# Chunked SSD scan: two products moved from GpSimd to VectorE, and the decode steps' order constraint dropped

## The chip, the cores and the metric

One core of one Trainium2 chip. The metric is the device time of one execution of the whole program in microseconds; a kernel's time is the median of several runs. Everything is f32 in memory; the large products run on TensorE as three f32r products each (high by high, high by low, low by high part).

## The reference

One inference step of a hybrid decoder layer, for a prompt of 1024 positions and for 8 decode sequences of one position each. The part around the change is the SSD scan (24 heads of 64, 4 groups of B and C, state 64, chunks of 128 positions):

```python
    acum = jnp.cumsum(dtc * a.reshape(G, R), axis=2)
    ...
    y_diag = jnp.einsum('bclsgr,bcsgrp->bclgrp', mix, xc)
    chunk_states = jnp.einsum('bclgn,bclgr,bclgrp->bcgrpn', bc, decay_to_end * dtc, xc)
    chunk_decay = jnp.exp(acum[:, :, -1])
    def step(h, inp):
        cs, cd = inp
        return cd[..., None, None] * h + cs, h
    ...
    y_off = jnp.einsum('bclgn,bcgrpn,bclgr->bclgrp', cc, h_in, jnp.exp(acum))
    y = y_diag + y_off
```

The decode sequences do one step of the same recurrence on a state that is read from memory and written back. Before the scan stand a projection and a causal convolution of x, B and C; behind it the gate SiLU(z), a grouped norm, the pooling groups, the output projection and the feed-forward part.

## The kernel before, in words

The program has a startup, the scans of the prompt beside the input projection (`ssd_phase`, line 754), a stage with the rest of the gates and the pooling groups, the output projection, and the feed-forward part with its up and down projection. The scans lie between about 137 and 396 us of the profiled execution.

`ssd_phase` makes a queue of small tasks and lets the projection's tiles (`conv_tile`, `gate_tile`, products L159 to L161) call `between` ahead of each of their three column blocks; `between` takes tasks from the queue by a credit. So the scan's steps lie between the projection's products. There are two scans, `ssd_tasks(0)` and `ssd_tasks(1)`, with 12 heads and two groups of B and C each. A scan has eight chunks. `step(c)` applies chunk c (`apply`), prepares the products of chunk c + 1 (`turn`) and the exponentials of chunk c + 2 (`decay`).

- `decay` (line 529) loads the cumulated logarithms of the decay in a broadcast form, clamps them on VectorE (L538), and takes 12 exponentials on ScalarE (called through L188) for `mix`. For c > 0 it takes the exponentials `ce` too and multiplies them with C (L553, GpSimd). `mix` and `ce` have two buffers.
- `turn` (line 556) transposes B and x on TensorE (L565, L574), makes the product of C and B (L571), copies and scales them on VectorE (L575, L576, L578) and multiplies `mix` with the product of C and B on VectorE (L583, two per chunk).
- `apply` (line 588) makes the chunk's state on TensorE (L597, in the single bank pM), multiplies the old state with its decay (L606, GpSimd), adds the two (L610, VectorE), and makes the output in the banks pY from `mix` and x (L620) and from `ce` and the old state (L630). VectorE adds the skip term (L638).

`sample_tile` (line 653) is one decode step for two heads of all 8 sequences: it loads B and C (L662, when they change) and a state (L666), and does 13 or so small operations on GpSimd alone (L670 to L682, with the write of the state at L674). The tiles of a step have one buffer each, so the steps follow one another. Seven steps belong to `ssd_phase`: 0 to 2 are queued behind the first scan, 3 to 6 after chunks 0, 2, 4 and 6 of the second. The helper `sample` (line 796) puts all GpSimd instructions of a step behind `self.pl`, the last L606 traced so far. Five further steps lie in the next stage, without this. Other work of GpSimd in the scans: the low parts of the weights during the first scan (L141; VectorE does them in the second), small copies for the convolution (L494, L495, L511) and sums of the grouped norm (L714).

The order of the instructions on each engine is not written out by hand. A scheduler orders them when the program is built (`TileContext(nc, schedule_with_timeline_sim=True)`, line 1589), by an expected time at which each is ready; on the chip each engine then runs its list in that order. `behind(ins)` (line 175) adds an order to it: what is traced in its block and runs on the engine of `ins` is put behind `ins` in that engine's list. It is no wait for a result.

Of the kernel before, what the change touches and what calls it, by code (L numbers as in the profile page):

```python
# [13 lines left out]
ALU = mybir.AluOpType  # L14
# [4 lines left out]
P = 128  # L19
# [56 lines left out]
class Kernel:  # L76
    def __init__(self, ctx, tc, d):
        self.ctx, self.tc, self.nc, self.d = ctx, tc, tc.nc, d
        nc = self.nc
        pool = lambda name, bufs=1, **kw: ctx.enter_context(tc.tile_pool(name=name, bufs=bufs, **kw))  # L80
        self.const = pool("const")
        self.wpool = pool("weights")
        self.big = pool("big", 30)
        self.dram = pool("scratch", 1, space=DRAM)

        self.cst = self.const.tile([P, NCONST], F32, name="cst")
        self.mat = self.const.tile([P, NMAT], F32, name="mat")
        self.conv_st = self.const.tile([P, 16, 35], F32, name="conv_st")
        self.ones = self.const.tile([P, P], F32, name="ones")
        nc.vector.memset(self.ones, 1.0)  # L90
        self.zero = self.const.tile([P, P], mybir.dt.bfloat16, name="zero")
        nc.vector.memset(self.zero, 0.0)
        self.eps = self.const.tile([P, 1], F32, name="eps")
        nc.gpsimd.memset(self.eps, EPS)
        self.ident = self.mat[:, M_ID : M_ID + P]
        self.uid = 0
        self.lo_eng = nc.vector
        self.hooks = []
        self.pl = None
        self.tab = self.set = None  # L100
        self.table_set(EXPLN)

# [426 lines left out]
    def decay(self, q, c):  # L529

        nc = self.nc
        h0 = 12 * q
        mix = self.ph.tile([P, 12, P], F32, tag="mix", name=self.nm("mix"), bufs=2)
        src = lambda h, n, p: self.acd[c : c + 1, h * P : (h + n) * P].partition_broadcast(p)
        nc.sync.dma_start(mix.rearrange("p r l -> p (r l)"), src(h0, 12, P))
        hs = c * NH + h0

        nc.vector.scalar_tensor_tensor(  # L538
            out=mix, in0=self.acl[:, hs : hs + 12].unsqueeze(2).broadcast_to([P, 12, P]), scalar=80.0, in1=mix,
            op0=ALU.subtract, op1=ALU.max,  # L540
        )
        ce = None
        if c > 0:
            ce = self.ph.tile([P, 6, P], F32, tag="ce", name=self.nm("ce"), bufs=2)
            for g in range(2):
                rows = slice(64 * g, 64 * g + 64)
                nc.sync.dma_start(ce[rows].rearrange("p r l -> p (r l)"), src(h0 + 6 * g, 6, 64))
        for r in range(12):
            self.tables(mix[:, r], mix[:, r], AF.Exp, bias=self.acl[:, hs + r : hs + r + 1], scale=-1.0)
        if c > 0:  # L550
            self.tables(ce, ce, AF.Exp, scale=-1.0)
            cc = self.ctl[q][:, c * P : (c + 1) * P]
            nc.gpsimd.tensor_tensor(out=ce, in0=ce, in1=cc.unsqueeze(1).broadcast_to([P, 6, P]), op=ALU.mult)  # L553
        return mix, ce

    def turn(self, q, c, mix):
# [31 lines left out]
    def apply(self, q, c, mix, ce, xd, bT):  # L588

        nc = self.nc  # L590
        cols = slice(c * P, (c + 1) * P)
        h = self.hst.get(q)
        halves = [slice(0, 64), slice(64, 128)]
        pys = [self.bank("pY") for _ in range(2)]
        pst = self.bank("pM")
        for g, rows in enumerate(halves):
            nc.tensor.matmul(  # L597
                pst[rows, :384], bT[:, rows], xd[:, 1, 6 * g : 6 * g + 6].rearrange("p r x -> p (r x)"),
                start=True, stop=True,
            )  # L600
        h1 = self.ph.tile([P, 384], F32, tag="h", name=self.nm("h"), bufs=2)
        if c == 0:
            nc.scalar.activation(h1, pst[:, :384], AF.Copy)
        else:
            by_head = lambda t: t.rearrange("p (r x) -> p r x", x=64)
            self.pl = nc.gpsimd.tensor_tensor(  # L606
                out=by_head(h1), in0=by_head(h),
                in1=self.cd[:, c, q].unsqueeze(2).broadcast_to([P, 6, 64]), op=ALU.mult,
            ).ins
            nc.vector.tensor_tensor(out=h1, in0=h1, in1=pst[:, :384], op=ALU.add)  # L610
        self.hst[q] = h1
        if c == NCH - 1:
            nc.sync.dma_start(self.d["ssm_p"][q], h1)

        for g in range(2):
            for i in range(3):
                o = slice(i * P, (i + 1) * P)
                for j, out in enumerate(halves):
                    r = 6 * g + 2 * i + j
                    nc.tensor.matmul(  # L620
                        pys[g][out, o], xd[:, 0, r, :], mix[:, r, :], start=(i == 0), stop=(c == 0 and i == 2),
                        skip_group_check=True,
                    )

        for i in range(3 if c > 0 else 0):
            o = slice(i * P, (i + 1) * P)
            for j, out in enumerate(halves):
                r = 2 * i + j
                for g, rows in enumerate(halves):
                    nc.tensor.matmul(  # L630
                        pys[g][out, o], h[rows, r * 64 : (r + 1) * 64], ce[rows, r, :], start=False, stop=(i == 2),
                        skip_group_check=True,
                    )
        for g in range(2):
            for i in range(3):
                k = 6 * q + 3 * g + i
                t = self.xs[k][:, cols]
                nc.vector.scalar_tensor_tensor(  # L638
                    out=t, in0=t, scalar=self.c("dsk", k), in1=pys[g][:, i * P : (i + 1) * P],
                    op0=ALU.mult, op1=ALU.add,  # L640
                )
# [112 lines left out]
    def ssd_phase(self):  # L754
        nc, d = self.nc, self.d
        self.hst = {}
        self.tags = {"bc": ("bc", 1), "st": ("st", 1), "stt": ("stt", 1), "dx": ("dx", 2)}
        queue = []

        credit = [0.0, 0.0]  # L760

        def between():
            credit[0] += credit[1]
            while credit[0] >= 1.0 and queue:
                credit[0] -= 1.0
                queue.pop(0)()
            if not queue:
                credit[0] = 0.0

        def flush():  # L770
            while queue:
                queue.pop(0)()

        def ssd_tasks(q):
            dec, trn = {}, {}

            def start():
                dec[0] = self.decay(q, 0)

            def step(c):  # L780
                if c >= 0:
                    self.apply(q, c, *dec.pop(c), *trn.pop(c))
                if c + 1 < NCH:
                    trn[c + 1] = self.turn(q, c + 1, dec[c + 1][0])
                if c + 2 < NCH:
                    dec[c + 2] = self.decay(q, c + 2)
                if c == -1 and q == 0:
                    self.sample_bc(q)
                if q == 1 and c in (0, 2, 4, 6):
                    sample(3 + c // 2)  # L790

            queue.append(start)
            for c in range(-1, NCH):
                queue.append(lambda c=c: step(c))

        def sample(i):
            with self.behind(self.pl):
                self.sample_tile(i // 6, i)

        self.lo_eng = nc.gpsimd  # L800
        for n in range(1, 6):
            self.keep(n, self.conv_tile(n, n, None))
        ssd_tasks(0)
        credit[:] = 0.35, 0.6
        for n in (13, 15, 6, 7, 8, 9):
            self.keep(n, self.conv_tile(n, n, between))
        flush()
        self.lo_eng = nc.vector
        self.sample_bc(1)
        for i in range(3):  # L810
            queue.append(lambda i=i: sample(i))
        credit[1] = 0.7
        for n in (10, 11):
            self.keep(n, self.conv_tile(n, n, between))
        nc.sync.dma_start(d["conv_o"], self.conv_st)

        ssd_tasks(1)
        self.gate_tile(16, 0, between)
        credit[:] = 0.35, 0.6
        for i in range(1, 7):  # L820
            self.gate_tile(16 + i, i, between)
        flush()
        self.run_due()
# [789 lines left out]
```

## Time and profile before

| | |
|---|---|
| median of 3 runs | 1409.85 us (1405.99 to 1411.67) |
| profiled execution, its own time | 1407.76 us |
| its span, first to last instruction | 1406.0 us |
| mean granted clock of TensorE, share of full | 0.984 |
| VectorE busy | 991.2 us (70%) |
| ScalarE busy | 700.6 us (50%) |
| GpSimd busy | 561.5 us (40%) |

In the rows below PE is TensorE, PEld its weight load, DVE VectorE, ACT ScalarE, POOL GpSimd. L553 is line 553 of the kernel. A busy time is from an instruction's start to its end and includes what it lost to others while it ran. The names are the program's tiles, without buffer numbers: `ce` and `mix` are the exponentials, `h` the state, `wop` the parts of the weights, `pT`, `pM`, `pY` and `g` banks that TensorE writes.

### The profile page before, as it was taken

To read this page: it belongs to the slowest core of one execution; us is meant where nothing else is said; L and a number is where in the kernel's file an instruction comes from. 1 tells how busy PE (TensorE), PEld (TensorE's weight loads), DVE (VectorE), ACT (ScalarE), POOL (GpSimd) and SP (SyncE) were. 2 spreads that over 40 slices of the span, in tenths; PEclk is the share of its full clock that TensorE was granted. 3 is DMA by queue.
4 is the path that set the end of the run, shared out by engine and by line. 5 is a ranking of instruction groups with operands and counts; after the bars stand their busy time and mean duration, and the time that the engine had idled before them with its cause. 6 is when DMAs were issued, how large, how long until landed. Compare 5 with 4: busy or idle time off the path is not lost. (4 is left out here: it accounts for less than half of the span.)

```text
span 1406.0 us, 26779 instructions
## 1 busy us (share of the span) xinstructions
PE 1360.4 (97%) x10360; PEld 1312.9 (93%) x10360; DVE 991.2 (70%) x1453; ACT 700.6 (50%) x1408; POOL 561.5 (40%) x704
## 2 busy tenths in 40 slices
PE   8999999979999999999979999999999999999997
PEld 7799879968799999899979999999999999999997
DVE  6575898669865684844689877777776787567743
ACT  6346774546644451311456545554554465444452
POOL 4233465888668305774222212212222224214122
PEclk9999999989999999999999999999999999999999
DMA  6031235243331256675477877777777769657513
GB/s 248 1 108 38 93 118 168 81 142 116 94 104 62 74 192 209 214 253 178 152 204 148 210 205 193 187 207 183 185 187 201 196 207 328 225 185 235 180 55 121
DMA packets 117820, 228.09 MB, mean 162 GB/s; under 512 B 19884, under 2 KB 37116, under 8 KB 117692
## 3 DMA queue, kind: packets, MB, share of 16 engines
q1 hardware_dynamic: 73772, 130.21, 29.3%
q0 software_dynamic: 27056, 70.22, 19.8%
q10 hardware_dynamic: 16864, 25.95, 5.6%
q8 instruction: 81, 1.33, 0.4%
q14 instruction: 47, 0.39, 0.1%
HBM read 169.64 MB, written 45.15 MB: 153 GB/s over the span
## 5 line engine op out<-in xcount | busy, mean ns | idle before, releaser
L1118 PE MATMUL g<-op,wop 128*128 128x258 f32 x3696 | 446.9, 283 | 4.3 <-DVE op L1048 1.6
L1118 PEld LDWEIGHTS g<-op,wop 128*128 128x128 f32 x3696 | 445.3, 189 | 5.6 <-DVE op L1048 2.0
L140 ACT ACTIVATE wop<-raw 128x512 fp32r<-128x512 f32 (+1 forms) x208 | 125.9, 608 | 231.2 <-PE g L161 139.7
L1300 PE MATMUL g<-op,wop 128*128 128x258 f32 x1848 | 224.9, 283 | 1.6 <-ACT op L210 0.9
L159 PE MATMUL g<-hh,wop 128*128 128x344 f32 x696 | 226.1, 325 | 0.0
L160 PE MATMUL g<-hl,wop 128*128 128x344 f32 x696 | 225.3, 324 | 0.0
L1300 PEld LDWEIGHTS g<-op,wop 128*128 128x128 f32 x1848 | 222.5, 189 | 2.7 <-ACT op L210 1.1
L161 PE MATMUL g<-hh,wop 128*128 128x344 f32 x696 | 224.8, 323 | 0.0
L141 DVE TENSOR_TENSOR wop<-raw,wop 128x512 fp32r<-128x512 f32 (+1 forms) x186 | 159.7, 862 | 83.3 <-ACT wop L140 81.5
L140 ACT ACTIVATE wop<-s 128x512 fp32r<-128x512 f32 (+1 forms) x136 | 83.6, 620 | 137.6 <-PE g L1300 51.9
L1098 POOL DMA_DIRECT2D s<-s x44 | 37.7, 857 | 249.8 <-DVE wop L141 89.2
L159 PEld LDWEIGHTS g<-hh,wop 128*128 128x128 f32 x696 | 132.2, 190 | 1.2 <-issue 1.1
L161 PEld LDWEIGHTS g<-hh,wop 128*128 128x128 f32 x696 | 132.1, 190 | 1.2 <-issue 1.2
L160 PEld LDWEIGHTS g<-hl,wop 128*128 128x128 f32 x696 | 132.1, 190 | 0.5 <-issue 0.4
L1200 DVE SCALAR_TENSOR_TENSOR acc<-u,cst,acc 128x1048 f32<-128x1048 f32 x88 | 115.2, 1309 | 12.2 <-ACT acc L1198 10.6
L141 DVE TENSOR_TENSOR wop<-s,wop 128x512 fp32r<-128x512 f32 (+1 forms) x136 | 92.1, 682 | 36.5 <-ACT wop L140 34.1
L1178 DVE TENSOR_TENSOR u<-u,g 128x258 f32<-128x258 f32 (+2 forms) x176 | 58.0, 354 | 72.2 <-PE g L1118 67.6
L1175 ACT ACTIVATE u<-g 128x258 f32<-128x258 f32 (+2 forms) x220 | 69.6, 340 | 71.2 <-PE g L1118 71.2
L160 PE MATMUL g<-yl,wop 128*128 128x344 f32 x288 | 93.4, 325 | 3.2 <-DVE yl L211 3.2
L161 PE MATMUL g<-yh,wop 128*128 128x344 f32 x288 | 93.0, 323 | 0.0
L159 PE MATMUL g<-yh,wop 128*128 128x344 f32 x288 | 92.9, 323 | 0.0
L1270 POOL DMA_DIRECT2D g<-td x77 | 41.2, 539 | 123.1 <-DVE op L211 70.2
(276 smaller groups left out, 2333.9 us busy)
## 6 DMA issues: line engine op xcount, KB each, us to landing
s<-wup SPq DMA_DIRECT2D x88, 256.0 KB, 3.2
g<-td POOLq DMA_DIRECT2D x77, 258.0 KB, 4.5
raw<-wup SPq DMA_DIRECT2D x66, 256.0 KB, 4.1
raw<-win SPq DMA_DIRECT2D x58, 256.0 KB, 2.7
mix<-acd SPq DMA_DIRECT2D x16, 768.0 KB, 4.5
td<-acc ACTq DMA_DIRECT2D x22, 516.0 KB, 6.1
s<-wup POOLq DMA_DIRECT2D x44, 256.0 KB, 5.3
s<-s POOLq DMA_DIRECT2D x44, 256.0 KB, 3.9
```

The lines of the kernel that those rows point to most:

```text
L140: self.nc.scalar.activation(hi, raw[:, :w], AF.Copy)
L141: lo_eng.tensor_tensor(out=lo, in0=raw[:, :w], in1=hi.bitcast(F32), op=ALU.subtract)
L159: nc.tensor.matmul(ps[:, :n], wh, xh[:, sl], start=(first and k == 0), stop=False)
L160: nc.tensor.matmul(ps[:, :n], wh, xl[:, sl], start=False, stop=False)
L161: nc.tensor.matmul(ps[:, :n], wl, xh[:, sl], start=False, stop=(final and k == last))
L1098: nc.gpsimd.dma_start(t, raw[acc] if acc in raw else w[acc][j], accum_op=ALU.add)
L1118: nc.tensor.matmul(out, a, b, start=(p in OPENS and j == 1), stop=(j == 12), skip_group_check=True)
L1175: a = nc.scalar.activation(out, ps[:, s], AF.Copy, scale=-1.0 if p in ("p5", "p4") else 1.0)
L1178: nc.vector.tensor_tensor(out=out, in0=out, in1=ps[:, s], op=op)
L1200: nc.vector.scalar_tensor_tensor(out=acc, in0=u[:, k : k + FW], scalar=self.c("fw", 3 * n + k), in1=acc, op0=ALU.mult, op1=ALU.add)
L1270: self.loaded = self.nc.gpsimd.dma_start(st[:, j], self.td[i + j][ROW[p]]).ins
L1300: self.pe = nc.tensor.matmul(out, a, b, start=(s == 0 and i == 0 and j == 0), stop=(s == len(PIECES) - 1 and i == nk - 1 and j == 2),).ins
```

## The change

The product of `ce` with C (L553) and the product of the old state with its decay (L606) are issued on VectorE in place of GpSimd. The field `self.pl` goes, and with it the order that put the seven decode steps of `ssd_phase` behind an L606.

```diff
@@ __init__
-        self.pl = None
@@ decay
             cc = self.ctl[q][:, c * P : (c + 1) * P]
-            nc.gpsimd.tensor_tensor(out=ce, in0=ce, in1=cc.unsqueeze(1).broadcast_to([P, 6, P]), op=ALU.mult)
+            nc.vector.tensor_tensor(out=ce, in0=ce, in1=cc.unsqueeze(1).broadcast_to([P, 6, P]), op=ALU.mult)
@@ apply
-            self.pl = nc.gpsimd.tensor_tensor(
+            nc.vector.tensor_tensor(
                 out=by_head(h1), in0=by_head(h),
                 in1=self.cd[:, c, q].unsqueeze(2).broadcast_to([P, 6, 64]), op=ALU.mult,
-            ).ins
+            )
             nc.vector.tensor_tensor(out=h1, in0=h1, in1=pst[:, :384], op=ALU.add)
@@ ssd_phase
         def sample(i):
-            with self.behind(self.pl):
-                self.sample_tile(i // 6, i)
+            self.sample_tile(i // 6, i)
```

## Rows read from the trace of the kernel before

**Rows 1.** The page, busy time by engine, and TensorE in 40 slices.
```profile
PE 1360.4 (97%) x10360; PEld 1312.9 (93%) x10360; DVE 991.2 (70%) x1453; ACT 700.6 (50%) x1408; POOL 561.5 (40%) x704
...
PE   8999999979999999999979999999999999999997
```

**Rows 2.** Waits of TensorE, 137 to 396 us: us in total, times, longest.
```profile
PE pY L630 <- POOL ce L553: 9.8, 2, 9.2
PE pM L565 <- DVE h L610: 3.7, 4, 1.9
PE pY L620 <- DVE mix L583: 2.9, 2, 2.1
PE pT L571 <- DVE cb L576: 2.8, 1, 2.8
...
```

**Rows 3.** Table by stretch: length; PE, PEld, DVE, ACT, POOL busy; PEclk; DMA.
```profile
159.50:162.90 3.40, 3.40 (x14) 3.40 (x14) 3.40 (x8) 3.38 (x8) 1.66 (x1) 0.51 0.52 154
...
296.10:302.90 6.80, 6.80 (x43) 4.97 (x45) 2.33 (x7) 0.00 (x0) 6.15 (x11) 0.50 0.10 39
337.10:340.40 3.30, 3.30 (x13) 3.08 (x13) 3.30 (x2) 1.99 (x7) 2.38 (x2) 0.50 0.32 118
...
```

**Rows 4.** Timeline, 276 to 305 us: start, length, [idle before and its releaser].
```profile
279.37 0.83 ACT L188 ACTIVATE ce<-ce 128x768 f32<-128x768 f32 x1
...
285.01 0.94 DVE L583 TENSOR_TENSOR mix<-mix,cb 128x768 f32<-128x768 f32 x1
...
287.66 3.61 ACT L188 ACTIVATE mix<-mix,acl 128x128 f32<-128x128 f32 x12 [1.04 <-DVE mix L538]
...
290.18 0.60 POOL L666 DMA_DIRECT2D st<-st_ssm  x1
...
293.24 1.03 POOL L672 TENSOR_TENSOR st<-st,dA 128x512 f32<-128x512 f32 x1 [2.45 <-DMA st<-st_ssm]
294.24 1.79 POOL L553 TENSOR_TENSOR ce<-ce,xs 128x768 f32<-128x768 f32 x1
...
296.08 1.54 PE L630 MATMUL pY<-ce,h 64*64 64x128 f32 x12 [9.19 <-POOL ce L553]
...
304.10 0.95 DVE L583 TENSOR_TENSOR mix<-mix,cb 128x768 f32<-128x768 f32 x1
```

**Rows 5.** Groups by line, VectorE and GpSimd, 137 to 396 us.
```profile
L583 DVE TENSOR_TENSOR mix<-mix,cb 128x768 f32<-128x768 f32 x32 | 41.7, 1304 | 1.9 <-ACT mix L188 1.9
...
L610 DVE TENSOR_TENSOR h<-h,pM 128x384 f32<-128x384 f32 x14 | 7.6, 545 | 5.2 <-PE pM L597 3.0 <-POOL st L680 2.2
...
L553 POOL TENSOR_TENSOR ce<-ce,xs 128x768 f32<-128x768 f32 x14 | 33.7, 2405 | 35.6 <-ACT ce L188 35.5
...
L606 POOL TENSOR_TENSOR h<-h,cd 128x384 f32<-128x384 f32 x14 | 18.7, 1337 | 12.5 <-DVE h L610 7.6 <-PE pY L630 4.9
```

**Rows 6.** Table by stretch, the first and the second scan; columns as in rows 3.
```profile
137.00:235.00 98.00, 93.88 (x821) 82.23 (x819) 91.79 (x132) 67.97 (x154) 57.08 (x45) 0.98 0.40 125
269.00:396.00 127.00, 111.50 (x888) 97.16 (x886) 103.64 (x148) 78.92 (x169) 96.09 (x101) 0.92 0.36 113
```

**Rows 7.** Timeline of VectorE and GpSimd, 330 to 335 us.
```profile
330.07 2.48 POOL L714 TENSOR_TENSOR sq<-sq,sq 128x1056 f32<-128x1056 f32 x1
330.13 5.25 DVE L141 TENSOR_TENSOR wop<-raw,wop 128x512 fp32r<-128x512 f32 x1
...
333.80 1.03 POOL L672 TENSOR_TENSOR st<-st,dA 128x512 f32<-128x512 f32 x1
```

**Rows 8.** Timeline of GpSimd, 240 to 364 us.
```profile
242.90 1.62 POOL L671 TENSOR_TENSOR stt<-bc,dx 128x512 f32<-128x512 f32 x1 [3.31 <-DMA bcd<-bcs]
...
352.68 0.21 POOL L682 TENSOR_TENSOR xs<-xs,dx 128x8 f32<-128x8 f32 x1
...
362.45 0.83 POOL L606 TENSOR_TENSOR h<-h,cd 128x384 f32<-128x384 f32 x1 [0.80 <-PE pY L630]
363.23 0.95 POOL L662 DMA_DIRECT2D bc<-bcd  x1
```

## The prediction

> **What bounds the kernel now.** I started from the page's busy shares: TensorE is busy 97% of the span, and 35 of the 40 slices show it at 9; of the other five one (281 to 316 us) lies in the scans [rows 1]. So whatever the change does on VectorE and GpSimd, it can pay only through the few places where TensorE stands still, or runs at its lower clock. The second view is TensorE's waits, restricted to the stretch with both scans (137 to 396 us) [rows 2]. The reader is to see that one wait stands out: 9.2 us in one piece, for the product of C with its exponentials (L553, GpSimd). The others are for VectorE: 3.7, 2.9 and 2.8 us. Together the four are 19.2 us; one further row, 0.3 us on L578, is left out, and there is no other.
>
> The third view is the table by stretch [rows 3], for the granted clock. Behind each of the four longest of these waits lies a stretch granted at 0.50 (1.2 GHz in place of 2.4): 3.4 us after an idle of 1.9 us, 6.8 us of work after the 9.2 us, and 3.3 us after the idle of 2.8 us (a like row of 3.3 us, after an idle of 2.1 us at 376, is not repeated). Work done there takes twice its time, so the four cost 1.7, 3.4, 1.7 and 1.7 us.
>
> The timeline around the long wait shows its cause [rows 4]. The exponentials were ready at 280.2 us (279.37 + 0.83). GpSimd, which runs its instructions in order, had decode steps ahead of the product: the load of a decode state issued at 290.18, then L672, which stood 2.45 us for that load, and L553 only at 294.24. TensorE began L630 at 296.08, after 9.19 us. The product itself took 1.79 us of the 16 us between ready and done; the rest was queue.
>
> **Product with C, moved to VectorE.** It leaves GpSimd with 14 x 2405 ns = 33.7 us [rows 5]. On VectorE no row has this instruction, but L583 has its shape and its broadcast (128x768 f32, both inputs in SBUF): 0.94 us bare [rows 4], 1.30 us on average over 32 [rows 5]. So it costs VectorE 14 x 0.94 = 13.2 us at least and 14 x 1.30 = 18.3 us at most; I take the lower end, since the average holds what GpSimd's load now adds.
>
> **State times its decay, moved to VectorE.** 14 x 1337 ns = 18.7 us leave GpSimd. L610, of the same 128x384, takes 545 ns: 14 x 0.545 = 7.6 us [rows 5]. Its other bound is half of 1.30 us, 14 x 0.65 = 9.1 us. It comes just ahead of L610 on the same engine, so no signal between engines is left in it; but where L610 is what TensorE waits for (3.7 us in 4 waits, all in the first scan), it may come 0.55 us later, at most 7 x 0.55 = 3.8 us in that scan. I take nothing there, because the old state is ready long before and VectorE may do the product in a pause; the 3.8 us stay as a bound.
>
> **VectorE's room.** Both together add 20.8 us (27.4 at most), half in each scan: about 10.4 us (13.7). VectorE is idle 98.0 - 91.8 = 6.2 us in the first scan and 127.0 - 103.6 = 23.4 us in the second [rows 6]. In the second it fits. In the first it does not fit by itself, but L583 alone loses 32 x (1.30 - 0.94) = 11.5 us over the two scans to something that is not its own work, and the timeline shows what that is [rows 7]: a product L141 of VectorE that began at 330.13 took 5.25 us, through back-to-back GpSimd instructions from 330.07 to 334.83, and the wait of 2.8 us on TensorE ends on the same VectorE queue (L576). In the first scan GpSimd's 57.1 us [rows 6] fall by half of 33.7 + 18.7, to about 31, so I expect a like share of this loss back: some 3 to 6 us. The balance of the first scan is then 10.4 - 6.2 - 3 to 6 us: between -2 and +1. I enter 0, with +3.8 us as upper bound and, below, the 3.7 us of waits and their 1.7 us of clock gone.
>
> **Decode steps released.** Seven steps lose a constraint on issue order, nothing else; it costs and saves no work. Each brings its instructions and its DMAs on GpSimd's queue (L662 twice where B and C change, L666, L674); SP's queue is passed by nothing. What really sets their order is shown in [rows 8]: the first of them waits at 242.90 for the rows of B and C that the second group's tiles only then deliver, and this stays. The last held one had its way free at 352.89 and was held until the state's product at 362.45; that is some 10 us earlier now, away from the end of the scan. I price the release at 0 us: in this stage only the gate of the same two heads reads what a step leaves (L700), and the view of TensorE's waits has none for it [rows 2]. What can move ahead of the 242.90 is a few preparations of the first steps; with a state load in front, L672 would hold GpSimd's weight products L141 for about the 2.45 us it now waits [rows 4]. TensorE does not wait for those products in this stretch at all [rows 2], so I enter 0 and keep 2.5 us as bound.
>
> **What is late next.** With the product on VectorE, L630 of that chunk could start at 286.9. But VectorE is working just there: L583, whose result starts the chunk's other products, ended at 285.95 [rows 4], and one more 0.94 us instruction ahead of it moves everything by that. So 1.0 us of the 9.2 stays. The next chunk needs its 12 exponentials, done at 287.66 + 3.61 = 291.3; its L583 ran at 304.10 and would be wanted some 12 us earlier, at 292. That just holds.
>
> **The sum.** The two waits on L553: -9.8 us. Left of them: +1.0. Clock behind the long one: -3.4. VectorE's queue in the first scan: 0. Release: 0. Total -12.2 us. The profiled execution took 1407.8 us (its span 1406.0), so 1395.6 us. The median of the runs shown is 2.1 us above the profiled one, 0.15%; I give 1396. After the scans three slices alone are below 9 [rows 1], so an earlier end of the scan is an earlier end of the kernel.
>
> **Rivals.** About 0.5% (7 us, 1402.8 to 1416.9 around the median) is what a measurement of this kernel can tell from no change.
>
> *VectorE's queue takes over.* The product now stands in order behind other work, and where ScalarE is late with the exponentials, everything behind it on VectorE (the next chunk's L575, L583, L610, L638) waits too. For it: GpSimd's wait for these exponentials is the product's main idle before it, 35.6 us [rows 5]; and the first scan has 6.2 us to spare. Against: VectorE waited only 1.9 us for ScalarE's exponentials ahead of L583 [rows 5]. At 0.5 us in each of 14 chunks (my choice, between nothing and 1 us) plus the 3.8 us it returns 10.8 us: 1406. The Trainium skill speaks for this one: "Perfetto Trace Analysis", section Optimizing Scalar/DVE Operations, warns that moving operations between VectorE and GpSimd might not help as they share an SBUF port; no row here shows such a move, and by that rule nothing is gained, 1408. Also here: that the released steps stay where they are and the product gains nothing, 1408.
>
> *Decode steps lock out VectorE (slower).* Place: the second scan, 290 to 350 us, where the released steps follow each other without the gaps that the state's products made. Mechanism: as in [rows 7], a chain of GpSimd instructions holds one VectorE instruction up. Price: 2.8 us of TensorE's idle [rows 2] and 1.7 us of clock [rows 3], 4.5 us. It decides from the fifth such event on: 1396 + 5 x 4.5 = 1418; in all seven chunks, 1427. For: VectorE now carries all that TensorE waits for. Against: one such event in the whole second scan now, and GpSimd's work there falls by 26 of 96 us. The Trainium skill, "SBUF — State Buffer", section SBUF: two separate sides, calls the shared port pair an exclusive lock held for a whole instruction; [rows 7] agree, with the 5.25 us.
>
> *VectorE's waits shrink as well (faster than forecast).* With GpSimd's load down by 52 us, the waits of the second scan on L576 and L583 (2.8 + 2.9 us) and the clock behind them (3.4 us) go too: 1396 - 9.1 = 1387.
>
> **How the numbers follow.** Forecast with its near bounds (1390 to 1402.8): 0.50. Faster still: 0.15. VectorE's queue takes over, or nothing changes: 0.22. Lock-out, slower: 0.13. So faster 0.65, same 0.22, slower 0.13. The range goes from 1385 (the third rival and 2 us) to 1412, through most of the case of no change; it leaves out the lock-out and the tails, under 0.2.
>
> **What would show it.** Right: no wait of L630 over 1.5 us, no stretch at 0.50 between 287 and 303 us, L553 on VectorE at about 0.95 us, GpSimd some 52 us less busy, VectorE some 10 to 20 us more, and the gap-free pace from the end of the scan 12 us earlier. Wrong: TensorE's waits on VectorE in the two scans growing beyond their 9.4 us, VectorE idle with ScalarE's exponentials as releaser ahead of L553, or VectorE instructions of several us beside chains of decode steps.

## The result: slower by 0.4%, and the profile after

Over 20 runs of each kernel the change takes 1413.3 us (1407.6 to 1417.0), the kernel before 1407.1 us (1399.9 to 1412.7). The ratio is 1.0044, 95% interval 1.0028 to 1.0059: slower, by some 6 us, where the prediction's sum had 12.2 us less. The profiled execution has a span of 1410.7 us, 4.7 us more than before. In the changed kernel the line numbers are one or two lower: L552 is the product with C, L605 the state's product, L713 the group sum, L692 the gate's copy, L669 to L681 a decode step. Decode steps are numbered from 0: step 3 is the fourth.

The first view of the changed kernel is the page: busy time by engine, TensorE in 40 slices, and the chain that ended last.

```profile
PE 1356.1 (96%) x10360; PEld 1307.3 (93%) x10360; DVE 990.1 (70%) x1481; ACT 701.3 (50%) x1408; POOL 523.1 (37%) x676
...
PE   8999999994999999899979999999999999999997
...
PE 75%; POOL 9%; DMA 6%; DVE 5%; issue 3%; ACT 1%; DVEq 0%; SPq 0%; POOLq 0%; ACTq 0%
```

GpSimd is 38 us less busy, VectorE is busy as long as before although it has 28 instructions more. One slice of TensorE (317 to 353 us) has fallen to 4. And the chain now runs for 9% of the span over GpSimd and for 6% over transfers; its lines there are those of the decode steps.

The waits of TensorE and of ScalarE in the same stretch as in [rows 2], 137 to 396 us (us in total, times, longest), name the place:

```profile
PE g L158 <- ACT z L692: 19.2, 1, 19.2
PE pM L564 <- DVE h L609: 3.3, 2, 2.5
PE pT L720 <- POOL sq L713: 1.4, 1, 1.4
PE pY L619 <- DVE mix L582: 0.4, 1, 0.4
PE pM L596 <- DVE xd L577: 0.2, 1, 0.2
...
ACT sq L711 <- POOL sq L713: 25.6, 1, 25.6
```

The wait for the product with C, 9.8 us in [rows 2], is gone. In its place stands a single wait of 19.2 us, which is in no row of before: TensorE cannot go on with a projection product (L158), because ScalarE has not copied an earlier one out of its bank (L692). ScalarE stands 25.6 us for the group sum (L713) on GpSimd.

The timeline of the changed kernel shows how the one hangs on the other, first GpSimd, then ScalarE and TensorE (start, length, idle before and its releaser); the last fence is the second square of the first norm in the kernel before:

```profile
315.19 0.58 POOL L665 DMA_DIRECT2D st<-st_ssm  x1
...
334.21 0.21 POOL L681 TENSOR_TENSOR xs<-xs,dx 128x8 f32<-128x8 f32 x1
334.36 0.58 POOL L665 DMA_DIRECT2D st<-st_ssm  x1
...
346.48 0.21 POOL L681 TENSOR_TENSOR xs<-xs,dx 128x8 f32<-128x8 f32 x1
346.62 0.58 POOL L665 DMA_DIRECT2D st<-st_ssm  x1
347.22 2.42 POOL L713 TENSOR_TENSOR sq<-sq,sq 128x1056 f32<-128x1056 f32 x1
```
```profile
316.73 1.07 ACT L711 ACTIVATE sq<-xs 128x1056 f32<-128x1056 f32 x1
...
323.26 0.83 ACT L187 ACTIVATE ce<-ce 128x768 f32<-128x768 f32 x1
349.67 1.08 ACT L711 ACTIVATE sq<-xs 128x1056 f32<-128x1056 f32 x1 [25.58 <-POOL sq L713]
350.66 0.79 ACT L692 ACTIVATE z<-g 128x344 f32<-128x344 f32 x2
...
351.15 0.65 PE L158 MATMUL g<-hh,wop 128*128 128x344 f32 x1 [19.24 <-ACT z L692]
```
```profile
327.50 1.08 ACT L712 ACTIVATE sq<-xs 128x1056 f32<-128x1056 f32 x1
```

GpSimd does decode step 4 (315 to 334), then step 5 (334 to 346.7), issues the load of step 6, and only then the first group sum, at 347.2. The second square, which this sum adds, had been done since 317.8: the sum stood 29 us in GpSimd's list. In the kernel before, it followed the second square by 1.5 us (328.58 to 330.07 [rows 7]). The grouped norm squares three tiles on ScalarE; the second and the third square share one buffer (`sq[1]`), so the third square (349.67) waits until the sum has read the second. ScalarE runs in order: behind the third square stand the gate's copies (350.66), and behind these TensorE.

The table by stretch, columns as in [rows 3], gives the granted clock and the two scans (the first row lies behind TensorE's wait of 2.5 us for L609):

```profile
315.20:318.40 3.20, 3.20 (x13) 3.20 (x12) 3.20 (x8) 3.17 (x4) 1.11 (x4) 0.50 0.96 344
335.70:351.10 15.40, 0.00 (x0) 0.00 (x0) 1.04 (x1) 1.43 (x3) 14.14 (x19) 0.50 0.29 85
351.20:356.10 4.90, 4.90 (x14) 3.04 (x14) 3.94 (x2) 4.90 (x17) 4.50 (x5) 0.50 0.33 97
...
137.00:235.00 98.00, 97.14 (x849) 85.41 (x848) 90.99 (x143) 70.15 (x159) 28.49 (x24) 1.00 0.37 114
269.00:396.00 127.00, 103.16 (x848) 88.33 (x847) 99.51 (x150) 73.08 (x157) 77.37 (x86) 0.91 0.33 107
```

The clock fell while TensorE stood and stayed at 0.50 (1.2 GHz) for 4.9 us of work. The projection's products started 0.29 us apart there, and 0.16 us apart just before the wait, so about 2 us were lost. The first scan is better than before: TensorE 97.1 of 98 us busy at full clock, against 93.9 at 0.98 [rows 6].

The same can be put as a race. The projection's products stand in the same order in both kernels; the table takes the start of the n-th of them, counted from the start of the program, and how far three kernels were ahead (-) or behind (+) of the kernel before at it:

```
product   before at   changed   order given back   sums on VectorE
    840       192.2      -4.9               -4.4              -4.2
   1320       314.6     -18.2              -18.4             -17.3
   1440       348.5      +2.6               -6.9             -14.3
   1680       409.3      +1.7              -10.4             -15.7
   2160       489.0      +6.2               -8.8             -14.3
```

So the changed kernel was well ahead at product 1320 (not all 18 us are gain: a part is only another order of scan and projection on TensorE, and none of the three kernels keeps them). Within 34 us the lead was given back. Another 4.5 us go between 409 and 489 us, where the last grouped norm brings a wait of 2.6 us, for a sum on VectorE this time, and a stretch of lower clock.

### The profile page after: what moved, and what is told of

Same layout as the page of the kernel before. It is cut to its first block, busy times and chain, and to the rows that moved or that the text cites. A ratio compares the mean times of both kernels' runs of the same rounds, so it can differ in the third digit from the quotient of the medians.

```text
span 1410.7 us, 26736 instructions
## 1 busy us (share of the span) xinstructions
PE 1356.1 (96%) x10360; PEld 1307.3 (93%) x10360; DVE 990.1 (70%) x1481; ACT 701.3 (50%) x1408; POOL 523.1 (37%) x676
## 4 chain that ended last, share of the span: by engine, by line
PE 75%; POOL 9%; DMA 6%; DVE 5%; issue 3%; ACT 1%; DVEq 0%; SPq 0%; POOLq 0%; ACTq 0%
PE g L1116 30%; PE g L1298 15%; PE g L159 8%; PE g L160 8%; PE g L158 8%; POOL st L679 2%; DMA st<-st_ssm 2%; POOL stt L670 1%; POOL st L671 1%; POOL stt L672 1%; POOL st L674 1%; DMA ssm_s<-stt 1%; PE pY L619 1%; DMA bc<-bcd 1%; DVE wop L140 1%
## 5 line engine op out<-in xcount | busy, mean ns | idle before, releaser
L158 PE MATMUL g<-hh,wop 128*128 128x344 f32 x696 | 226.3, 325 | 19.2 <-ACT z L692 19.2
L140 DVE TENSOR_TENSOR wop<-raw,wop 128x512 fp32r<-128x512 f32 (+1 forms) x186 | 158.4, 858 | 85.7 <-ACT wop L139 83.3
L158 PEld LDWEIGHTS g<-hh,wop 128*128 128x128 f32 x696 | 132.3, 190 | 22.5 <-ACT z L692 19.5
L1198 DVE SCALAR_TENSOR_TENSOR acc<-u,cst,acc 128x1048 f32<-128x1048 f32 x88 | 115.2, 1309 | 12.2 <-ACT acc L1196 10.6
L140 DVE TENSOR_TENSOR wop<-s,wop 128x512 fp32r<-128x512 f32 (+1 forms) x136 | 92.2, 683 | 36.1 <-ACT wop L139 33.6
L158 PE MATMUL g<-yh,wop 128*128 128x344 f32 x288 | 92.6, 322 | 0.0
```

Source lines behind the costliest of these rows:

```text
L140: lo_eng.tensor_tensor(out=lo, in0=raw[:, :w], in1=hi.bitcast(F32), op=ALU.subtract)
L158: nc.tensor.matmul(ps[:, :n], wh, xh[:, sl], start=(first and k == 0), stop=False)
L1198: nc.vector.scalar_tensor_tensor(out=acc, in0=u[:, k : k + FW], scalar=self.c("fw", 3 * n + k), in1=acc, op0=ALU.mult, op1=ALU.add)
```

## The experiments

Theory A after the result: the moved products are worth what was forecast, and the released decode steps cost the difference to the measured time, because group sums stand behind them in GpSimd's list. Rival B: VectorE's new two-input instructions hold GpSimd up, so that its work is late in any order. All ratios are against the kernel before in the same session.

### One product alone, order kept

Only the line of `decay` in the diff is taken.

```diff
-            nc.gpsimd.tensor_tensor(out=ce, in0=ce, in1=...)
+            nc.vector.tensor_tensor(out=ce, in0=ce, in1=...)
```

> The product of C with its exponentials alone goes to VectorE; the state's product stays on GpSimd and the decode steps stay behind it. Theory A (the 19.2 us wait of the changed kernel comes from the group sums standing behind released decode steps in GpSimd's list; the moved product by itself is worth what was forecast): no wait of TensorE over 3 us, time 10 to 14 us under the kernel before, ratio 0.990 to 0.993. Rival B (VectorE's added two-input instructions hold GpSimd up, so that decode steps and group sums come late in whatever order): ratio 1.000 to 1.006, with GpSimd's decode instructions of several us and a wait of ScalarE for the group sum of over 10 us.

Measured: 1403.3 us, ratio 0.9973 (0.9952 to 0.9995). Both missed. The waits of TensorE (137 to 396 us), and GpSimd's timeline there:

```profile
PE pM L565 <- DVE h L610: 16.4, 6, 10.1
```
```profile
291.84 0.60 POOL L666 DMA_DIRECT2D st<-st_ssm  x1
298.03 1.03 POOL L672 TENSOR_TENSOR st<-st,dA 128x512 f32<-128x512 f32 x1 [5.59 <-DMA st<-st_ssm]
...
302.54 0.83 POOL L606 TENSOR_TENSOR h<-h,cd 128x384 f32<-128x384 f32 x1
```

The wait moved to the next thing that TensorE needs from GpSimd: the state's product, behind the same decode step and its load. It keeps the bank pM, and the next chunk's transposes wait 10.1 us for it.

### The release alone

```diff
-            with self.behind(self.pl):
-                self.sample_tile(i // 6, i)
+            self.sample_tile(i // 6, i)
```

> Both products stay on GpSimd, only the order behind the state's product is dropped. Theory A: the first group sum falls behind more decode work, ScalarE waits for it, and TensorE gets a wait on the gate's copy of 5 to 20 us: ratio 1.005 to 1.015. Rival B (the release does nothing by itself, the products on VectorE make GpSimd late): ratio 0.998 to 1.002 and no wait of TensorE on the gate's copy.

Measured: 1407.5 us, ratio 1.0010 (0.9989 to 1.0030). Theory A's number missed; by itself the release has no effect that 12 runs show (0.3% at most). Waits of TensorE, and the first group sum in GpSimd's timeline:

```profile
PE pM L565 <- DVE h L610: 11.1, 6, 4.1
PE pY L630 <- POOL ce L553: 9.7, 2, 9.2
```
```profile
336.92 2.43 POOL L714 TENSOR_TENSOR sq<-sq,sq 128x1056 f32<-128x1056 f32 x1
```

With the products still on GpSimd, its list has other instructions between those of a step, and the sum stands within step 5 (321 to 346 us), not behind it. The wait for the state's sum (L610) has grown from 3.7 to 11.1 us, while those on L583 and L576, 5.7 us in [rows 2], are gone. So the 15 us shown below are the price of the release together with the move, not of the release alone.

### The changed kernel with the order given back

```diff
+            self.pl = nc.gpsimd.tensor_copy(self.mark, h[:, 0:1]).ins
             nc.vector.tensor_tensor(
                 out=by_head(h1), in0=by_head(h), ...
...
-            self.sample_tile(i // 6, i)
+            with self.behind(self.pl):
+                self.sample_tile(i // 6, i)
```

> The changed kernel with the order given back: the decode steps stand behind a one-column GpSimd copy of the chunk's old state, in the place of the state's product. The copy (14 times, some 0.1 to 0.3 us each) is added work whose result nothing reads. Theory A: the group sums stand ahead of the sixth and seventh decode step again, no wait of TensorE over 3 us: 1393 to 1399, ratio 0.990 to 0.994. Rival B: as the changed kernel, ratio 1.003 to 1.006.

Measured: 1397.1 us, ratio 0.9938 (0.9915 to 0.9962). Rival B's number is out; A's ratio holds, its "no wait over 3 us" does not:

```profile
PE pM L566 <- DVE h L612: 5.0, 2, 4.2
PE pT L723 <- POOL sq L716: 4.6, 1, 4.6
```

With the order given back the same two moves come to 0.9938 in place of 1.0044, a difference of 1.06%, 15 us. A wait of 4.6 us for the group sum is left even so.

### Both products and the group sums on VectorE, decode steps free

```diff
-            eng = nc.gpsimd if g < 2 else nc.vector
+            eng = nc.vector
```

> The changed kernel, decode steps free, with the sums of squares of the first two grouped norms on VectorE as those of the last two are; four instructions of 1056 columns move. Theory A: the 19.2 us wait and 2.5 us of its clock go, 1390 to 1396, ratio 0.988 to 0.992, though GpSimd's decode steps are as late as in the changed kernel. Rival B: the late decode steps hold the gates instead (a gate's small product reads what the step leaves), a wait of 10 us or more stays somewhere behind GpSimd: ratio 0.998 to 1.006.

Measured: 1391.2 us, ratio 0.9894 (0.9866 to 0.9921): the changed kernel with four instructions moved, and faster than both kernels. The longest waits of TensorE:

```profile
PE pM L564 <- DVE h L609: 3.5, 3, 2.5
PE pM L596 <- DVE xd L577: 1.7, 2, 1.5
```

GpSimd's decode steps are as late as in the changed kernel, or later: step 3 ends at 316.1 us (315.3 there) and step 4 at 341.1 (334.4). Nobody waits for them.

### One step alone behind the sums

The changed kernel; only decode step 5 is put behind the second sum of the first grouped norm.

```diff
+            add = eng.tensor_tensor(out=sq[0], in0=sq[0], in1=sq[1], op=ALU.add).ins
+        if g == 0:
+            self.sums0 = add
...
-            self.sample_tile(i // 6, i)
+            with self.behind(self.sums0 if i == 5 else None):
+                self.sample_tile(i // 6, i)
```

> The changed kernel with one order alone: the sixth decode step (number 5) stands behind the second sum of the first grouped norm in GpSimd's list; the other six are free, both products on VectorE. Theory A (the 19.2 us come from the place of that sum behind the sixth step): the wait on the gate's copy goes, at most 5 us of another wait for the sum stay, 1391 to 1398, ratio 0.989 to 0.994. Rival B (GpSimd is late as a whole, whatever the order): a wait of 10 us or more stays, ratio 0.999 to 1.005.

Measured: 1398.0 us, ratio 0.9934 (0.9911 to 0.9958). This one place in the list is worth as much as the order of all seven steps (0.9938), as far as the runs can tell. The wait on the gate's copy is gone; its size for what remains was missed:

```profile
PE pT L722 <- POOL sq L713: 9.9, 1, 9.9
```

The sum now stands behind step 4 instead, and step 4 ends at 334.0. So the wait that is left comes from the lateness of GpSimd as such, rival B's part.

### The other product alone

As the run with the order given back, but the product with C stays on GpSimd.

```diff
-            nc.vector.tensor_tensor(out=ce, in0=ce, in1=...)
+            nc.gpsimd.tensor_tensor(out=ce, in0=ce, in1=...)
```

> The state's product alone on VectorE, the product of C with its exponentials back on GpSimd; the decode steps are held behind the one-column copy as in the run that gave the order back. Theory A (each of the two products, left on GpSimd, meets the same queue of decode steps, so that both must go): the wait of TensorE for the product with C stays at 7 to 10 us, ratio 0.997 to 1.001. Rival C (the state's product was the one that mattered, as the wait on the state's sum in the run with the other product alone suggests): ratio 0.992 to 0.996.

Measured: 1410.2 us, ratio 1.0027 (1.0002 to 1.0052). The wait is the expected one, the time a little above A's range; rival C is out.

```profile
PE pY L632 <- POOL ce L554: 9.5, 1, 9.5
```

A further wait of 4.8 us stands behind the scans, for a sum of the last grouped norm on VectorE (L716). With the first run of this section: the product with C alone gains 0.3%, the state's alone loses 0.3%, both together (order kept) gain 0.6%.

### Sums on VectorE with the order kept, and in the kernel before

Two controls. The first has both products and the sums on VectorE and the steps held behind the one-column copy; the second is the kernel before with the sums on VectorE.

```diff
-            eng = nc.gpsimd if g < 2 else nc.vector
+            eng = nc.vector
```

> Both products and all the sums of the grouped norms on VectorE, and the decode steps held behind the one-column copy. Theory A: nothing that TensorE waits for is left on GpSimd in the second scan, so the order of the decode steps no longer matters: within 3 us of the run with free steps and sums on VectorE, 1388 to 1394, ratio 0.987 to 0.992. If holding is worth something beyond the sums: under 1388.

> The kernel before, with the sums of the first two grouped norms on VectorE and nothing else changed. Theory A: no wait on these sums is in the trace of the kernel before, so ratio 0.997 to 1.002, and the 9.2 us wait for the product with C stays. Rival D (the sums on VectorE are a gain by themselves, with no link to the change): ratio 0.988 to 0.994.

Measured: 1391.9 us, ratio 0.9890 (0.9863 to 0.9916), and 1402.5 us, ratio 0.9974 (0.9951 to 0.9997). The longest waits of TensorE, of the one and of the other:

```profile
PE pM L566 <- DVE h L612: 5.6, 3, 4.2
```
```profile
PE pY L630 <- POOL ce L553: 6.0, 2, 4.8
```

Once nothing that TensorE waits for is left on GpSimd, the order of the decode steps is worth nothing that the runs can tell (0.9890 and 0.9894). In the kernel before, the sums on VectorE bring a quarter of a per cent; the wait for the product with C stays, but with 4.8 us in one piece in place of the 9.2 us that theory A expected, although the edit does not touch that product. The scheduler makes all lists anew for each kernel, so an edit can move more than its own lines. Rival D is out; a quarter of the gain of the changed kernel with its sums on VectorE (0.9894) may be the sums' own.

### Both products left out

The changed kernel without the two products on any engine (the exponentials are not multiplied with C, the old state is added without its decay), with the group sums on GpSimd and then on VectorE.

```diff
...
-            nc.vector.tensor_tensor(out=ce, in0=ce, in1=...)
...
-            nc.vector.tensor_tensor(out=by_head(h1), in0=by_head(h), ...)
-            nc.vector.tensor_tensor(out=h1, in0=h1, in1=pst[:, :384], op=ALU.add)
+            nc.vector.tensor_tensor(out=h1, in0=h, in1=pst[:, :384], op=ALU.add)
```

> The changed kernel without the two products on any engine: the exponentials are not multiplied with C, and the old state not with its decay. Decode steps free, group sums on GpSimd behind the sixth step as in the changed kernel. Theory E (the moved instructions themselves hold GpSimd up: 14 x 1.5 us more of two-input work on VectorE): the fourth decode step ends by 307 us (315.3 in the changed kernel, 302.8 before), the first group sum runs by 338, TensorE's wait for it is under 11 us, 1396 to 1403. Theory F (VectorE's other work, dense now that TensorE no longer stands still at 287, holds GpSimd up): the fourth step ends at 311 to 316, wait of 12 us or more, 1404 to 1412.

> The same without both products, and all group sums on VectorE: what is left of the scans when neither the two products nor the sums wait in GpSimd's queue. If the products are hidden on VectorE, as the sum of the prediction took it: 1387 to 1392, within 3 us of the run with free steps and sums on VectorE (1391.2). If VectorE's added 20.8 us are on the path for a part: 1378 to 1386.

Measured: 1403.8 us, ratio 0.9993 (0.9970 to 1.0015), and 1383.7 us, ratio 0.9852 (0.9805 to 0.9900). The longest waits, of the first and of the second:

```profile
PE pT L713 <- POOL sq L706: 18.9, 1, 18.9
```
```profile
PE pM L562 <- DVE h L602: 2.5, 3, 1.3
```

The first was to tell theory E (the moved instructions hold GpSimd up) from F (VectorE's other work does), and it does not decide. Step 3 takes 17.4 us (280.2 to 297.6), against 25.3 us in the changed kernel (290.0 to 315.3) and 12.6 us before (290.2 to 302.8), which speaks for a share of both. The three stretches do not hold quite the same work, though: before, the two products stand in it (2.6 us together), in the other two an instruction of step 4 (L670, 5.47 us in the changed kernel and 1.27 us here).

But it shows the main point once more. From the timelines of GpSimd and TensorE in the first of the two runs:

```profile
332.73 2.42 POOL L706 TENSOR_TENSOR sq<-sq,sq 128x1056 f32<-128x1056 f32 x1
...
343.72 2.40 POOL L706 TENSOR_TENSOR sq<-sq,sq 128x1056 f32<-128x1056 f32 x1
```
```profile
346.18 2.08 PE L713 MATMUL pT<-sq,ones 128*128 128x512 f32 x2 [18.94 <-POOL sq L706]
```

With no product on either engine, the first sum still stands behind step 5 (332.7 us), and the second behind nearly all of step 6 (343.7). TensorE, which came to its stop at 327.2 us here and at 331.9 us in the changed kernel, waits 18.9 us, until the second sum is done.

The second run gives the products' own price on VectorE: 0.9894 - 0.9852 = 0.4%, some 6 us. The two intervals overlap, so it is not shown that the price is above nothing.

## Why the prediction was wrong, point by point

**What bounds the kernel: right.** Over the runs, the time rises with TensorE's waits in the two scans, from 2.5 us of waits (1383.7 us) and 6.3 us (1391.2) to 24.5 us in the changed kernel (1413.3). It is no strict rule: with the products left out and the sums on GpSimd the waits are 21.2 us at 1403.8 us, before 19.5 us at 1407.1. VectorE took 28 more instructions without being busier. The prediction miscounted the slices of [rows 1]: 36 stand at 9, not 35, so the others are four, and two of them lie behind the scans, not three. Nothing in the sum hangs on it.

**The two moved products: right in price, nearly right in worth.** L552 and L605 took what L583 and L610 had promised (0.94 and 0.545 us), as these groups of the changed kernel show (137 to 396 us), and VectorE stood only 0.8 us for the exponentials:

```profile
L582 DVE TENSOR_TENSOR mix<-mix,cb 128x768 f32<-128x768 f32 x32 | 36.9, 1152 | 0.0
L552 DVE TENSOR_TENSOR ce<-ce,xs 128x768 f32<-128x768 f32 x14 | 13.3, 949 | 0.8 <-ACT ce L187 0.8
L605 DVE TENSOR_TENSOR h<-h,cd 128x384 f32<-128x384 f32 x14 | 7.9, 566 | 0.0
```

With the order kept they bring 0.9938, that is -8.7 us of 1407.1 (between -12.0 and -5.3), where the sum had -12.2. That the two belong together was not in the prediction: it took the whole 9.8 us for the product with C and nothing for the state's, and the single runs show that either one, left on GpSimd, meets the same queue.

**VectorE's room: right in the traces of the first scan, open over all.** GpSimd's load in the first scan fell to 28.5 us (31 forecast), L582 lost 32 x (1.152 - 0.94) = 6.8 us instead of 11.5, and the waits of the first scan shrank to 0.9 us with no lower clock: the lower bound that the prediction named. The run without the products puts their cost at some 6 us over both scans, where the sum had 0 and 1.0, but with intervals that overlap. GpSimd was to be some 52 us less busy and is 38 us, since its decode steps became longer; VectorE was to be 10 to 20 us busier and is not.

**Decode steps released, priced at 0: this step failed.** The prediction looked for readers of what a step leaves, found the gate alone, and took the order for free. The question it did not ask is what stands behind the steps in GpSimd's list. Those are the group sums, and the prediction's own text names GpSimd's in-order queue as the cause of the 9.2 us. It asked that question for the weight products (L141), and not for L714, whose rows [rows 7] quote. Nor did it follow the sum's one buffer to ScalarE, in whose list the gate's copies stand behind the third square. Cost: 15 us against the run that gave the order back, where the prediction had 0 and a bound of 2.5. It comes only together with the move: the release alone measured 1.0010.

**What is late next: missed.** The prediction checked the next chunk's exponentials, and these held: at product 1320 the changed kernel was 18.2 us ahead. Taking 9 us out of TensorE made everything after it due 9 us earlier, GpSimd's sums too, and GpSimd did not become faster but slower: step 3 ended 12.5 us later than before.

**The rivals.** The slower side was given 0.13, as decode steps that lock out VectorE. The place was right (the second scan) and the culprit, the decode steps; the victim and the mechanism were not: one wait in a queue, not five lock-outs. The lock goes the other way, below. The range ended at 1412, the median is 1413.3.

**Open.** How much of GpSimd's lateness comes from the moved instructions and how much from VectorE's other work. How far the changed order of other instructions, which the scheduler chose anew in every run, adds to the smaller differences. Whether a buffer of its own for the third square would free ScalarE wasn't tried.

## What to carry to other kernels

Before an order between instructions is dropped, list what stands behind them on the same engine and when that is due, not only who reads their results; a constraint that seems to hold work back may be what keeps something urgent ahead of it. When a stall is taken out, everything behind it is due earlier by as much: check each engine's list there, and each buffer that has a single copy. An engine with long background work should hold nothing that the main chain waits for, whether it is a product, a state or a sum; moved one at a time, the wait passes to the next of them, and most of the gain shows only with the last (0.9973 and 1.0027 for one product, 0.9938 for both, 0.9894 with the sums).

## What the runs showed of the hardware

VectorE can hold GpSimd up over several of its instructions, as GpSimd held VectorE in [rows 7]. From the timeline of the changed kernel:

```profile
294.85 5.36 POOL L671 TENSOR_TENSOR st<-st,dA 128x512 f32<-128x512 f32 x1 [3.54 <-DMA st<-st_ssm]
```
```profile
294.35 0.95 DVE L577 TENSOR_TENSOR xd<-xd,wd 128x768 f32<-128x768 f32 x1
...
296.95 1.75 DVE L537 SCALAR_TENSOR_TENSOR mix<-acl,mix 128x1536 f32<-128x1536 f32 x1
298.62 0.68 DVE L140 TENSOR_TENSOR wop<-raw,wop 128x512 fp32r<-128x512 f32 x1
299.22 0.54 DVE L609 TENSOR_TENSOR h<-h,pM 128x384 f32<-128x384 f32 x1
```

L671 takes 1.03 us when alone [rows 4]. Here VectorE ran five instructions with two SBUF inputs back to back, from 294.35 to 299.3 (L577, L582, the moved L552, L537, L140); L671 ended at 300.2, 1.0 us after L609 began, which reads one of its inputs from PSUM. This agrees with the exclusive lock that the Trainium skill states ("SBUF — State Buffer", section SBUF: two separate sides), and adds that the loser did not get its turn here between two instructions of the other engine. The load of a decode state also took longer: 4.8 us from issue to release at 290.03, against some 3 us before [rows 4]; no run here tells why.
